# Up projection of a diffusion block on one core: the upper weight part multiplies both token parts in one matmul of 512 columns

## The chip, the cores and the metric

The kernel runs on one core of one Trainium2 chip. The metric is the time of one execution on the device, in microseconds. Five engines work side by side and meet through semaphores: TensorE (PE for its matmuls, PEld for its weight loads), VectorE (DVE), ScalarE (ACT), GpSimd (POOL) and SyncE (SP), whose queue issues the weight transfers here.

## The reference

One layer of a diffusion block over 256 latent tokens with 256 context tokens, model width 2048. The part that the change touches is the MLP, with a hidden width of 8192:

```python
def squared_relu_mlp(h, w_up, w_down):
    return jnp.square(jax.nn.relu(h @ w_up)) @ w_down

hm = modulate(rms_norm(x, norm_mlp_w[layer]), sh_m, sc_m)
x = x + g_m * squared_relu_mlp(hm, w_mlp_up[layer], w_mlp_down[layer])
```

Ahead of it stand the adaLN products (`w_ada`), the input projection, a windowed attention with a pooling mixer beside it, and the output projection.

## The kernel before, in words

All large products are float32, computed as three products of two-part operands: a number is split into a rounded upper part (`hi`, type float32r) and the rest (`lo`), and `mm3` (L278) adds a[0]·b[0] (L280), a[0]·b[1] (L281) and a[1]·b[0] (L282) into one PSUM bank. Here a is the stationary operand (128 x 128, loaded into TensorE by a LDWEIGHTS of its own ahead of each matmul), b the moving one.

Weights come as one ordered stream of 1 MB tiles (`WeightStream`, L52): SP issues the loads five tiles deep (`N_RAW`), and each tile is split in two halves of 128 x 1024, the upper part by ScalarE (`hi`, L89), the lower part by VectorE, now and then GpSimd (`lo`, L91), six halves deep (`N_HALF`). A half's buffer comes free when TensorE has used the half, so a split usually starts when TensorE lets go of an old half.

The MLP stands at the end, from about 424 us on. The 8192 hidden columns go in 16 groups of 512; a group has four sums `m` of 128 hidden columns by 256 tokens and runs over 16 row blocks `k`. The first three groups are computed together (`first_up_groups`, L873). The other 13 go through `up_group` (L863): for each of four weight tiles, for each `m`, for each of the tile's four row blocks, one `mm3` with the weights stationary and the tokens' parts `mhi`, `mlo` (128 x 256 each) moving. So a position (group, `k`, `m`) costs three matmuls of 256 columns, and the weights' upper part is loaded twice. The tokens' parts are allocated by `parts` (L565), which also serves the attention and the pooling, and written by `modulate_m` (L841).

`activation` (L852) makes a group's four sums into the operand of the down projection: ScalarE's Relu out of PSUM (L857), VectorE's square (L858), then the two parts `ahi` (ScalarE, L859) and `alo` (VectorE, L860). `down_group` (L902) multiplies two groups' activations, as stationary operands, with 512 columns of `w_down`, 48 matmuls of 512 columns. The loop at L929 goes over blocks `b`: for b = 0 the first two groups, for b = 1 the third one and one `up_group`, for b = 2 to 7 two `up_group`s each, and each time four `down_group`s (`dg`).

A scheduler sets the order on each engine: it may move an instruction ahead of others of its engine in the program's text where data permit, so a matmul whose operand comes late can stand behind later ones.

Of the kernel before, what the change touches and what calls it, by code (L numbers as in the profile page):

```python
# [15 lines left out]
P = 128  # L16
D = 2048
# [10 lines left out]
# among the first so many tiles of the stream, GpSimd computes every third lower part  # L28
POOL_SPLITS = 140

# adaLN parts beyond the attention's shift and scale, in order of use: 512 columns of its gate ("g")
# or 256 of the MLP's scale and of its shift ("m"); the engine that multiplies them; and between
# which steps their tiles go, four for each
# [11 lines left out]
# groups of row blocks of w_out in their order of use: those of the pooling are ready first  # L45
OUT_ORDER = (0, 1, 2, 3)

# row blocks of w_in that are used at a time: (first, number)
# [3 lines left out]
class WeightStream:  # L52
    """One ordered stream of float32 weight tiles of four blocks [128, 512].

    Tiles are loaded in order, N_RAW deep. Those of the main products are split
    ahead of their use, two blocks at a time, into two float32r parts
    (hi + lo == w exactly).
    """
# [6 lines left out]
    def add(self, kind, *loads, halves=2):  # L65
        """loads: (view of the tile, source)."""
        if kind == "w":
            self.halves += [(len(self.items), h) for h in range(halves)]
        self.items.append((kind, loads, halves))
# [25 lines left out]
    def next(self, kind):  # L95
        """The next tile: the raw one, or W(j, cols) -> the parts of block j."""
        i = self.pos
        assert self.items[i][0] == kind, (i, self.items[i][0], kind)
        self.pos += 1
        self.load_to(i + N_RAW)  # L100
        self.split_to(self.n_used + N_AHEAD)
        raw = self.raw.pop(i)
        if kind != "w":
            return raw
        n = self.items[i][2]
        self.n_used += n
        halves = [self.split.pop((i, h)) for h in range(n)]

        def parts(j, cols=slice(0, 512)):
            hi, lo = halves[j // 2]  # L110
            return hi[:, j % 2, cols], lo[:, j % 2, cols]

        return parts
# [3 lines left out]
def kernel(  # L117
# [17 lines left out]
    # ------------------------------------------------------------ weight stream  # L135
# [15 lines left out]
    # the input projection's schedule, with the first shift and scale in pairs of row blocks  # L151
# [50 lines left out]
    # the last group's q goes before the attention, its u beside it  # L202
# [45 lines left out]
    # ------------------------------------------------------------ constants  # L248
# [10 lines left out]
    # ------------------------------------------------------------ small helpers  # L259
    def rstd(pool, ss, n):  # L260
        """1 / sqrt(ss / D + EPS) of ss [128, n], or of the sum of two."""
# [16 lines left out]
    def mm3(ps, a, b, first, last):  # L278
        """ps (+)= a^T b with a and b in two parts each."""
        nc.tensor.matmul(ps, a[0], b[0], start=first, stop=False, skip_group_check=True)  # L280
        nc.tensor.matmul(ps, a[0], b[1], start=False, stop=False, skip_group_check=True)  # L281
        nc.tensor.matmul(ps, a[1], b[0], start=False, stop=last, skip_group_check=True)  # L282

    def ada_pe(finish):
        """Steps that multiply silu(c), silu(c_ctx) with 512 columns of w_ada on TensorE; a last one calls finish(e).

        Rows 32 j and 32 j + 1 of e hold partial sums.
        """
# [18 lines left out]
    def ada_dve(finish):  # L307
        """The same for silu(c) alone on VectorE: the sum of the rows of e is the result."""
# [14 lines left out]
    def ada_cols(e, weights):  # L323
        """e^T weights: the result with the columns on the partitions, PSUM [128, 4, 2]."""
# [5 lines left out]
    def ada_scale(dst, ps, bc, wc):  # L330
        """dst [128, n, 2] = w * (1 + scale)."""
# [6 lines left out]
    # ------------------------------------------------------------ norm of x and ctx  # L338
# [38 lines left out]
    def ada_attn(c_):  # L377
        """Scale and shift of the row blocks 2 c_ and 2 c_ + 1."""
# [11 lines left out]
    def normalize(i):  # L390
        """Tokens 128 i .. of x | ctx over their root mean square, transposed."""
# [24 lines left out]
    # ------------------------------------------------------------ input projection  # L416
# [15 lines left out]
    def modulated(c_, streams=(0, 1)):  # L432
        """The input projection's operand, in two parts, of the row blocks 2 c_ and 2 c_ + 1."""
# [79 lines left out]
    def run_late(n):  # L513
        """The next n steps; a chunk is finished one step after its last."""
        for _ in range(n):
            f = next(late_iter, None)
            while late_finish:
                late_finish.pop()()
            if f:
                f()  # L520
# [42 lines left out]
    # ------------------------------------------------------------ attention and pooling  # L563
# [4 lines left out]
    def parts(j):  # L568
        pool = mixa if j < 8 else mixb
        hi = pool.tile([P, T], F32R, tag=f"mhi{j}", name=f"mhi{j}", bufs=1)  # L570
        lo = pool.tile([P, T], F32R, tag=f"mlo{j}", name=f"mlo{j}", bufs=1)
        return hi, lo
# [10 lines left out]
    # masks of the two blocks: keys after the query (block 0), keys before it (block 1)  # L583
# [9 lines left out]
    def rotate(t):  # L593
        """Axial rotary of t [128, n, 256], in place."""
# [9 lines left out]
    def split_keys(g):  # L604
        """The two parts of the keys of group g, each on both halves of the partitions."""
# [10 lines left out]
    def split_queries(cc):  # L616
        """For the heads 2 cc and 2 cc + 1, one part on each half of the partitions."""
# [8 lines left out]
    def pool_mean(g):  # L626
        """Window mean minus the token itself, in place of u."""
# [25 lines left out]
    def pool_project(g):  # L653
# [7 lines left out]
        for d in range(2):  # L661
            mhi, mlo = parts(8 + 2 * g + d)
# [5 lines left out]
    # the attention of the heads 2 cc and 2 cc + 1 for the block qb of 128 queries, in stages  # L668
    class Unit:
# [14 lines left out]
        def maxima(self):  # L684
            """Masks, and the negated maxima of the scaled scores and the sink."""
# [35 lines left out]
    def attend(cc):  # L721
# [6 lines left out]
        mhi, mlo = parts(cc)  # L728
# [53 lines left out]
    # ------------------------------------------------------------ output projection  # L782
# [53 lines left out]
    # ------------------------------------------------------------ MLP  # L836
# [4 lines left out]
    def modulate_m(kg):  # L841
        """The up projection's operand, in two parts, of four row blocks."""
        for j in range(4):
# [3 lines left out]
            hi, lo = parts(k)  # L847
            nc.scalar.activation(hi, v, AF.Identity, bias=sm[:, k, 0:1])
            nc.vector.scalar_tensor_tensor(lo, v, sm[:, k, 0:1], hi.bitcast(F32), ALU.add, ALU.subtract)
            hm.append((hi, lo))  # L850

    def activation(pss):  # L852
        ahi = mp.tile([P, 4, T], F32R, tag="ahi", name="ahi", bufs=3)
        alo = mp.tile([P, 4, T], F32R, tag="alo", name="alo", bufs=3)
        for m in range(4):
            t = mp.tile([P, T], F32, tag="act", name="act", bufs=2)
            nc.scalar.activation(t, pss[m], AF.Relu)  # L857
            nc.vector.tensor_tensor(t, t, t, ALU.mult)  # L858
# [4 lines left out]
    def up_group():  # L863
        pss = [bank("ps_up")[:, 0:T] for _ in range(4)]
        for kg in range(4):
            w = S.next("w")
            for m in range(4):
                for j in range(4):
                    k = 4 * kg + j
                    mm3(pss[m], w(j, slice(P * m, P * m + P)), hm[k], k == 0, k == KC - 1)  # L870
        return activation(pss)

    def first_up_groups():  # L873
        """Three groups at once, by row blocks, so that the last shifts and scales can come late.

        Two sums share a bank: the first product of the bank starts both.
        """
# [24 lines left out]
    def down_group(b, dg, acts, done=None):  # L902
        """Sums of 8 row blocks for 512 columns; done: called with each token block's as it is ready."""
# [37 lines left out]
    # last block: x2 + g * y is ready before its sums are  # L941
# [50 lines left out]
def _shape_constants():  # L992
    """Rotary tables [128, 2, 256] (cos, signed sin) and window size over tokens in the window at the two ends."""
# [40 lines left out]
```

## Time and profile before

| | |
|---|---|
| median of 3 runs | 1180.92 us (1180.76 to 1180.92) |
| span of the profiled execution | 1180.8 us |
| PE busy | 1128.4 us (96%) |
| DVE busy | 806.4 us (68%) |
| ACT busy | 509.2 us (43%) |
| granted TensorE clock, mean | 0.982 |

The profiled execution's span and the runs' median are 0.1 us apart; the profile names no time of its own beyond the span. A matmul's duration in a row (0.28 us for 256 columns) is longer than the distance from its start to the next one's start, since matmuls overlap in the array: what a stream of them costs is read from the starts. Clock 1.00 is 2.4 GHz, 0.50 is 1.2 GHz.

### The profile page before, as it was taken

How to read it: one execution, taken by the hardware profiler on the slowest of the kernel's cores; microseconds unless marked ns; L12 is line 12 of the kernel's file. 1: busy time of each engine (PE TensorE's matmuls, PEld its weight loads, DVE VectorE, ACT ScalarE, POOL GpSimd, SP SyncE). 2: the span in 40 equal slices, each digit the busy share in tenths (PEclk: the TensorE clock that was granted, in tenths of full speed). 3: DMA queues.
4: the chain of work that ended last, by engine and by line, in shares of the span. 5: the costliest groups of instructions: out<-in, count | busy, mean ns of one | idle time of the engine just before them, and what ended most of it. 6: DMA issues, size and time to landing. Idle time of an engine off the chain costs nothing.

```text
span 1180.8 us, 17728 instructions
## 1 busy us (share of the span) xinstructions
PE 1128.4 (96%) x7140; PEld 952.2 (81%) x7140; DVE 806.4 (68%) x1203; ACT 509.2 (43%) x760; POOL 145.8 (12%) x98
## 2 busy tenths in 40 slices
PE   3999999989999979999999999999999999999996
PEld 2767788746588769988989989989989989988984
DVE  4645468988698888897765765774554554576576
ACT  4633233277633433365434434533533533543452
POOL 1111123610143312320000000000000000000001
PEclk9899999999999979899999999999999999999998
DMA  9999898577898899968675775775566555565532
GB/s 338 312 336 342 279 326 276 178 268 263 272 350 278 288 328 322 319 229 284 243 278 179 249 263 184 254 262 178 179 191 193 187 178 181 185 195 189 179 107 72
DMA packets 174017, 286.75 MB, mean 243 GB/s; under 512 B 5608, under 2 KB 72352, under 8 KB 172784
## 3 DMA queue, kind: packets, MB, share of 16 engines
q1 hardware_dynamic: 172800, 279.55, 70.7%
q0 software_dynamic: 848, 5.55, 1.3%
q8 instruction: 56, 0.92, 0.3%
q10 hardware_dynamic: 288, 0.52, 0.1%
q14 instruction: 25, 0.20, 0.0%
HBM read 283.50 MB, written 2.10 MB: 242 GB/s over the span
## 4 chain that ended last, share of the span: by engine, by line
PE 74%; DVE 13%; DMA 7%; issue 3%; ACT 1%; SPq 1%; POOL 1%; DVEq 0%; ACTq 0%
PE ps_d L282 10%; PE ps_d L281 10%; PE ps_d L280 10%; PE ps_up L282 9%; PE ps_up L280 9%; PE ps_up L281 9%; PE ps_ada L297 4%; DVE ada_v L319 4%; DVE lo L91 4%; DMA raw<-in_w_in_dram 2%; PE ps_qu L280 2%; DMA raw<-in_w_mlp_up_dram 2%; DMA raw<-in_w_out_dram 2%; PE ps_qu L282 2%; PE ps_qu L281 2%
## 5 line engine op out<-in xcount | busy, mean ns | idle before, releaser
L91 DVE TENSOR_TENSOR lo<-raw,hi 128x1024 fp32r<-128x1024 f32 x293 | 376.7, 1300 | 233.5 <-ACT hi L89 233.3
L89 ACT CAST hi<-raw 128x1024 fp32r<-128x1024 f32 x330 | 337.7, 1049 | 416.6 <-PE ps_d L282 159.4
L280 PE MATMUL ps_up<-mhi,hi 128*128 128x256 f32 x1024 | 292.0, 287 | 0.6 <-ACT hi L89 0.6
L282 PE MATMUL ps_up<-mhi,lo 128*128 128x256 f32 x1024 | 289.5, 285 | 1.4 <-DVE lo L91 1.4
L281 PE MATMUL ps_up<-mlo,hi 128*128 128x256 f32 x1024 | 290.1, 284 | 0.0
L281 PE MATMUL ps_d<-lo,ahi 128*128 128x512 f32 x512 | 200.5, 394 | 0.0
L280 PE MATMUL ps_d<-hi,ahi 128*128 128x512 f32 x512 | 200.5, 394 | 0.0
L280 PEld LDWEIGHTS ps_up<-mhi,hi 128*128 128x128 f32 x1024 | 197.4, 193 | 2.7 <-issue 1.8
L282 PE MATMUL ps_d<-hi,alo 128*128 128x512 f32 x512 | 199.5, 395 | 0.0
L282 PEld LDWEIGHTS ps_up<-mhi,lo 128*128 128x128 f32 x1024 | 196.8, 193 | 2.2 <-DVE lo L91 2.1
L281 PEld LDWEIGHTS ps_up<-mlo,hi 128*128 128x128 f32 x1024 | 197.5, 193 | 1.1 <-issue 1.0
L319 DVE SCALAR_TENSOR_TENSOR ada_v<-raw,c_sil,ada_v 128x512 f32<-128x512 f32 x135 | 124.7, 923 | 22.0 <-DMA raw<-in_w_ada_dram 20.1
L91 POOL TENSOR_TENSOR lo<-raw,hi 128x1024 fp32r<-128x1024 f32 x37 | 95.4, 2580 | 336.4 <-ACT hi L89 316.9
L282 PEld LDWEIGHTS ps_d<-hi,alo 128*128 128x128 f32 x512 | 96.5, 188 | 22.4
L280 PEld LDWEIGHTS ps_d<-hi,ahi 128*128 128x128 f32 x512 | 96.5, 188 | 22.2
L281 PEld LDWEIGHTS ps_d<-lo,ahi 128*128 128x128 f32 x512 | 96.5, 188 | 22.1
L280 PE MATMUL ps_qu<-hhi,hi 128*128 128x256 f32 x256 | 75.6, 296 | 5.9 <-ACT hhi L447 5.9
L297 PE MATMUL ps_ada<-raw,c_sil 128*32 128x512 f32 x480 | 74.3, 629 | 2.0 <-DMA raw<-in_w_ada_dram 1.9
L281 PE MATMUL ps_qu<-hlo,hi 128*128 128x256 f32 x256 | 72.7, 285 | 0.0
L282 PE MATMUL ps_qu<-hhi,lo 128*128 128x256 f32 x256 | 72.1, 285 | 0.0
L950 POOL DMA_DIRECT2D fw<-in_final_norm_w_dram x1 | 0.6, 571 | 576.3 <-DVE lo L91 576.3
L280 PEld LDWEIGHTS ps_qu<-hhi,hi 128*128 128x128 f32 x256 | 49.4, 193 | 24.4 <-issue 11.5
(189 smaller groups left out, 1275.2 us busy)
## 6 DMA issues: line engine op xcount, KB each, us to landing
raw<-in_w_ada_dram SPq DMA_DIRECT2D x128, 512.0 KB, 7.7
raw<-in_w_mlp_up_dram SPq DMA_DIRECT2D x64, 1024.0 KB, 5.5
raw<-in_w_mlp_down_dram SPq DMA_DIRECT2D x64, 1024.0 KB, 5.1
raw<-in_w_ada_dram SPq DMA_DIRECT2D x32, 1024.0 KB, 6.6
raw<-in_w_in_dram SPq DMA_DIRECT2D x19, 1024.0 KB, 6.7
raw<-in_w_out_dram SPq DMA_DIRECT2D x16, 1024.0 KB, 7.0
xnat<-in_x_dram SPq DMA_DIRECT2D x2, 1024.0 KB, 6.1
xnat<-in_ctx_dram SPq DMA_DIRECT2D x2, 1024.0 KB, 12.2
```

Of the source, the lines that this page charges most:

```text
L89: nc.scalar.copy(hi, raw)
L91: eng.tensor_tensor(lo, raw, hi.bitcast(F32), ALU.subtract)
L280: nc.tensor.matmul(ps, a[0], b[0], start=first, stop=False, skip_group_check=True)
L281: nc.tensor.matmul(ps, a[0], b[1], start=False, stop=False, skip_group_check=True)
L282: nc.tensor.matmul(ps, a[1], b[0], start=False, stop=last, skip_group_check=True)
L297: nc.tensor.matmul(ps[32 * j : 32 * j + 32, :], c_sil[:, 4 * kg + j, :], raw[:, j, :], start=(kg == 0), stop=(kg == 3), tile_position=(0, ...
L319: nc.vector.scalar_tensor_tensor(box["e"], raw[:, j, :], sc, box["e"], ALU.mult, ALU.add)
L950: nc.gpsimd.dma_start(out=fw, in_=final_w.partition_broadcast(P))
```

## The change

The two parts of a token block become one tile of 128 x 2 x 256 (`both`), `hi` in its first 256 columns and `lo` in the next. In `up_group` the weights' upper part multiplies the whole tile in one matmul of 512 columns, which fills a bank: the product with `hi` in the first half, that with `lo` in the second. The weights' lower part multiplies `hi` (256 columns) into the first half. `activation` adds the halves: ScalarE copies the second half to SBUF, VectorE adds the first one, and a second instruction of VectorE takes the positive part and squares it; the split into `ahi` and `alo` stays. `first_up_groups` keeps `mm3` and the old branch of `activation`. Comments and docstrings fall away too.

```diff
     def parts(j):
         pool = mixa if j < 8 else mixb
-        hi = pool.tile([P, T], F32R, tag=f"mhi{j}", name=f"mhi{j}", bufs=1)
-        lo = pool.tile([P, T], F32R, tag=f"mlo{j}", name=f"mlo{j}", bufs=1)
-        return hi, lo
+        both = pool.tile([P, 2, T], F32R, tag=f"mx{j}", name=f"mx{j}", bufs=1)
+        return both[:, 0, :], both[:, 1, :], both.rearrange("p a t -> p (a t)")
...
-            hi, lo = parts(k)
+            hi, lo, both = parts(k)
...
-            hm.append((hi, lo))
+            hm.append((hi, lo, both))
...
-            nc.scalar.activation(t, pss[m], AF.Relu)
-            nc.vector.tensor_tensor(t, t, t, ALU.mult)
+            if pss[m].shape[1] == T:
+                nc.scalar.activation(t, pss[m], AF.Relu)
+                nc.vector.tensor_tensor(t, t, t, ALU.mult)
+            else:
+                nc.scalar.copy(t, pss[m][:, T : 2 * T])
+                nc.vector.tensor_tensor(t, pss[m][:, 0:T], t, ALU.add)
+                nc.vector.scalar_tensor_tensor(t, t, 0.0, t, ALU.max, ALU.mult)
...
     def up_group():
-        pss = [bank("ps_up")[:, 0:T] for _ in range(4)]
+
+        pss = [bank("ps_up") for _ in range(4)]
         for kg in range(4):
             w = S.next("w")
             for m in range(4):
                 for j in range(4):
                     k = 4 * kg + j
-                    mm3(pss[m], w(j, slice(P * m, P * m + P)), hm[k], k == 0, k == KC - 1)
+                    hi, lo = w(j, slice(P * m, P * m + P))
+                    nc.tensor.matmul(pss[m], hi, hm[k][2], start=k == 0, stop=False, skip_group_check=True)
+                    nc.tensor.matmul(pss[m][:, 0:T], lo, hm[k][0], start=False, stop=k == KC - 1, skip_group_check=True)
         return activation(pss)
```

The order of every engine up to the first `up_group` is the one of before; from there on it moves at three kinds of places. First TensorE inside an `up_group` (`ps_up` is a sum, `hi` and `lo` the weights' parts, `mhi12`, `mlo12`, `mx2` and so on the tokens'), before:

```order
L280 MATMUL ps_up_7835<-mhi12_4703,hi_7897 128x256
L281 MATMUL ps_up_7835<-mlo12_4704,hi_7897 128x256
L282 MATMUL ps_up_7835<-mhi12_4703,lo_7898 128x256
L280 MATMUL ps_up_7835<-mhi13_4708,hi_7897 128x256
L281 MATMUL ps_up_7835<-mlo13_4709,hi_7897 128x256
L282 MATMUL ps_up_7835<-mhi13_4708,lo_7898 128x256
```

and now:

```order
L876 MATMUL ps_up_7930<-mx2_4037,hi_7863 128x512
L877 MATMUL ps_up_7930<-mx2_4037,lo_7864 128x256
L876 MATMUL ps_up_7930<-mx3_4041,hi_7863 128x512
L877 MATMUL ps_up_7930<-mx3_4041,lo_7864 128x256
L876 MATMUL ps_up_7927<-mx4_4230,hi_7893 128x512 [waits Activation_49]
L877 MATMUL ps_up_7927<-mx4_4230,lo_7894 128x256 [waits DVE_49]
```

Two matmuls stand where three stood, of lengths that alternate. Second, VectorE around the end of a block's second `up_group`, from b = 4 on; before:

```order
L858 TENSOR_TENSOR act<-act 128x256 x2
L860 TENSOR_TENSOR alo<-act,ahi 128x256 x2
L858 TENSOR_TENSOR act<-act 128x256
L91 TENSOR_TENSOR lo<-raw,hi 128x1024
L860 TENSOR_TENSOR alo<-act,ahi 128x256
L91 TENSOR_TENSOR lo<-raw,hi 128x1024
L858 TENSOR_TENSOR act<-act 128x256
L860 TENSOR_TENSOR alo<-act,ahi 128x256
```

and now:

```order
L861 TENSOR_TENSOR act<-ps_up,act 128x256 x2
L862 SCALAR_TENSOR_TENSOR act<-act 128x256 x2
L864 TENSOR_TENSOR alo<-act,ahi 128x256 x2
L91 TENSOR_TENSOR lo<-raw,hi 128x1024
L861 TENSOR_TENSOR act<-ps_up,act 128x256
L91 TENSOR_TENSOR lo<-raw,hi 128x1024
L861 TENSOR_TENSOR act<-ps_up,act 128x256
L862 SCALAR_TENSOR_TENSOR act<-act 128x256 x2
L864 TENSOR_TENSOR alo<-act,ahi 128x256
L91 TENSOR_TENSOR lo<-raw,hi 128x1024
L864 TENSOR_TENSOR alo<-act,ahi 128x256
```

The fourth sum's `alo` is last in both; now four more instructions and one more weight split of `lo` stand in the stretch. Third, TensorE in the `down_group`s right behind: the last first use of the second group's `alo` (row block 3, the row with the last DVE wait) stood 40 matmuls behind the first `ps_d`, before:

```order
L280 MATMUL ps_d1_8896<-hi_8817,ahi_8873 128x512
L281 MATMUL ps_d1_8896<-lo_8818,ahi_8873 128x512
L282 MATMUL ps_d1_8896<-hi_8817,alo_8874 128x512
L280 MATMUL ps_d1_8896<-hi_8817,ahi_8873 128x512
L280 MATMUL ps_d0_8895<-hi_8821,ahi_8873 128x512 [waits Activation_49]
L281 MATMUL ps_d0_8895<-lo_8822,ahi_8873 128x512
L281 MATMUL ps_d1_8896<-lo_8818,ahi_8873 128x512
L282 MATMUL ps_d0_8895<-hi_8821,alo_8874 128x512 [waits DVE_49]
```

and now 51 behind it, with matmuls of the next 512 columns (`ps_d0_8395`) drawn in ahead:

```order
L280 MATMUL ps_d0_8323<-hi_8261,ahi_8297 128x512 [waits Activation_49]
L281 MATMUL ps_d0_8323<-lo_8262,ahi_8297 128x512
L280 MATMUL ps_d1_8324<-hi_8261,ahi_8297 128x512
L281 MATMUL ps_d1_8324<-lo_8262,ahi_8297 128x512
L280 MATMUL ps_d0_8395<-hi_8327,ahi_8099 128x512
L281 MATMUL ps_d0_8395<-lo_8328,ahi_8099 128x512
L282 MATMUL ps_d0_8323<-hi_8261,alo_8298 128x512 [waits DVE_49]
```

The place is 51 matmuls behind for b = 4 to 7, 60 for b = 2 and 3 (before: 41), 55 for b = 1 (before: 40). GpSimd's and SP's orders do not move.

## Rows read from the trace of the kernel before

**Rows 1.** The page: busy time of the engines, and the chain by line.

```profile
PE 1128.4 (96%) x7140; PEld 952.2 (81%) x7140; DVE 806.4 (68%) x1203; ACT 509.2 (43%) x760; POOL 145.8 (12%) x98
...
PE ps_d L282 10%; PE ps_d L281 10%; PE ps_d L280 10%; PE ps_up L282 9%; PE ps_up L280 9%; PE ps_up L281 9%; PE ps_ada L297 4%; DVE ada_v L319 4%; DVE lo L91 4%; DMA raw<-in_w_in_dram 2%; PE ps_qu L280 2%; DMA raw<-in_w_mlp_up_dram 2%; DMA raw<-in_w_out_dram 2%; PE ps_qu L282 2%; PE ps_qu L281 2%
```

**Rows 2.** Windows of the MLP: length; each engine's busy time (instructions); clock; DMA.

```profile
core 0: us, PE busy (x) PEld busy (x) DVE busy (x) ACT busy (x) POOL busy (x), PEclk, DMA share, GB/s
622.74:714.28 91.54, 91.54 (x580) 82.61 (x579) 59.95 (x74) 38.52 (x49) 0.00 (x0) 1.00 0.69 230
```

**Rows 3.** Windows, instructions on `ps_up` alone: two groups of b = 5.

```profile
896.90:942.98 46.08, 46.08 (x384) 46.02 (x383) 2.68 (x7) 1.00 0.56 184
```

**Rows 4.** Windows, instructions on `ps_d` alone: the four `down_group`s of b = 5.

```profile
942.98:987.50 44.52, 44.52 (x192) 35.98 (x192) 4.82 (x7) 0.00 (x0) 1.00 0.60 187
```

**Rows 5.** Timeline, PE: both ends of that stretch (start us, us, operation).

```profile
942.86 0.28 PE L282 MATMUL ps_up<-mhi,lo 128*128 128x256 f32 x1
942.98 0.39 PE L280 MATMUL ps_d<-hi,ahi 128*128 128x512 f32 x1
...
987.36 0.40 PE L282 MATMUL ps_d<-hi,alo 128*128 128x512 f32 x1
987.59 0.28 PE L280 MATMUL ps_up<-mhi,hi 128*128 128x256 f32 x1
```

**Rows 6.** Timeline, PE: output projection, first and last of 44 matmuls.

```profile
340.09 0.39 PE L282 MATMUL ps_w<-hi,mlo 128*128 128x512 f32 x1
...
349.84 0.39 PE L280 MATMUL ps_w<-hi,mhi 128*128 128x512 f32 x1
```

**Rows 7.** Timeline, PE: values of the input projection, first and last of 11 matmuls.

```profile
148.04 0.28 PE L281 MATMUL ps_v<-lo,hhi 128*128 128x256 f32 x1
...
149.17 0.28 PE L282 MATMUL ps_v<-hi,hlo 128*128 128x256 f32 x1
```

**Rows 8.** Timeline, PE: one matmul of 512, six of 256, then 512 again.

```profile
95.20 0.39 PE L280 MATMUL ps_k<-hhi,hi 128*128 128x512 f32 x1
95.43 0.28 PE L281 MATMUL ps_v<-lo,hhi 128*128 128x256 f32 x1
...
96.14 0.40 PE L281 MATMUL ps_k<-hlo,hi 128*128 128x512 f32 x1
96.38 0.40 PE L282 MATMUL ps_k<-hhi,lo 128*128 128x512 f32 x1
```

**Rows 9.** Groups by line and shape: busy us, mean ns, idle before.

```profile
L857 ACT ACTIVATE act<-ps_up 128x256 f32<-128x256 f32 x64 | 24.3, 382 | 33.4 <-PE ps_up L282 24.1 <-DVE alo L860 9.0 <-PE ps_up L281 0.2
L858 DVE TENSOR_TENSOR act<-act 128x256 f32<-128x256 f32 x64 | 28.5, 455 | 9.5 <-ACT act L857 8.3
L849 DVE SCALAR_TENSOR_TENSOR mlo<-x2T,sm,mhi 128x256 fp32r<-128x256 f32 x16 | 6.9, 477 | 0.2 <-ACT mhi L848 0.2
L730 DVE TENSOR_TENSOR mlo<-ps_o,mhi 128x256 fp32r<-128x256 f32 x8 | 3.3, 418 | 3.6 <-ACT mhi L729 3.6
L729 ACT CAST mhi<-ps_o 128x256 fp32r<-128x256 f32 x8 | 3.0, 378 | 9.8 <-PE ps_o L726 9.1 <-DMA raw<-in_w_ada_dram 0.7
```

**Rows 10.** Timeline, DVE and ACT: the activation of b = 2, whose sums end at 669.21.

```profile
668.62 1.05 ACT L89 CAST hi<-raw 128x1024 fp32r<-128x1024 f32 x1 [0.27 <-PE ps_up L281]
673.58 1.05 ACT L89 CAST hi<-raw 128x1024 fp32r<-128x1024 f32 x1 [0.42 <-PE ps_d L282]
...
671.17 1.22 DVE L91 TENSOR_TENSOR lo<-raw,hi 128x1024 fp32r<-128x1024 f32 x1
674.18 0.42 DVE L860 TENSOR_TENSOR alo<-act,ahi 128x256 fp32r<-128x256 f32 x1
674.51 0.75 DVE L319 SCALAR_TENSOR_TENSOR ada_v<-raw,c_sil,ada_v 128x512 f32<-128x512 f32 x1
```

**Rows 11.** PE behind a wait in the first groups, and a window at half clock.

```profile
489.11 1.02 PE L327 MATMUL ps_adac<-ones,ada_v 128*128 128x2 f32 x8 [0.98 <-DVE ada_v L319]
490.50:497.30 6.80, 6.26 (x30) 5.97 (x29) 5.42 (x10) 0.91 (x2) 0.68 (x1) 0.50 1.00 352
```

More of the change, by code (lines that the diff above doesn't have):

```diff
@@ L661, in pool_project @@
         for d in range(2):
-            mhi, mlo = parts(8 + 2 * g + d)
+            mhi, mlo, _ = parts(8 + 2 * g + d)
             sc = cols[:, 64 + 2 * g + d : 65 + 2 * g + d]
@@ L727, in attend @@
                                  start=(k == 0), stop=(k == 3), tile_position=(0, 64 * i))
-        mhi, mlo = parts(cc)
+        mhi, mlo, _ = parts(cc)
         nc.scalar.copy(mhi, ps[:, 0:T])
```

## The prediction

> **What bounds the kernel now.** I read the page's busy time first, then its chain of waits: TensorE is busy 96% of the span, and the chain that ended last is mostly TensorE, with `ps_up` (27%) and `ps_d` (30%) as its largest parts [rows 1]. The page stands for the whole span, so I looked next at windows inside the MLP. From 622.74 to 714.28 us, a whole block of it, PE is busy for all of 91.54 us at clock 1.00, while VectorE has 59.95 and ScalarE 38.52 us of work and the DMA engines are at 0.69 [rows 2]. Nothing is waited for there: what a matmul costs from start to start is what the block costs.
>
> That cost is in the starts. Two groups are 384 matmuls of 256 columns in 46.08 us [rows 3], 120.0 ns each. The four `down_group`s of the same block are 192 of 512 columns from 942.98 to 987.59 us [rows 4, 5], 44.61 us, 232.3 ns each. At 2.4 GHz the columns alone would take 106.7 and 213.3 ns, so a matmul carries some 13 to 19 ns beside its columns, and a matmul less is worth that much, though the columns stay: 3 x 256 before, 512 + 256 now.
>
> The spacing is not one number. In the output projection 512 columns take (349.84 - 340.09) / 43 = 226.7 ns [rows 6], 13.3 above the columns, as with the 120.0 of `ps_up`; in a stretch of the value projection 256 columns take (149.17 - 148.04) / 10 = 113 ns [rows 7], 6 above them. All are at full clock and without idle time between, and go on unchanged through their stretches, so the fixed part depends on which operands a stream reads. The output projection reads the same buffers as the up projection (weight parts and the tiles of `parts`), with the roles of moving and stationary exchanged; so I take its 226.7 for the new matmul.
>
> **The change, part by part.**
>
> TensorE. 13 groups x 16 row blocks x 4 sums = 832 positions go through `up_group`. Before, one costs 3 x 120.0 = 360.0 ns [rows 3]. Now it costs one matmul of 512 and one of 256: 226.7 + 120.0 = 346.7 ns, 13.3 less. 832 x 13.3 ns = 11.1 us, all on the path, since PE has no idle time in the stage. The trace has one short stretch in which the lengths alternate without a pause: one of 512, six of 256, one of 512, from 95.20 to 96.38 us [rows 8], 1.18 us, where 2 x 226.7 + 6 x 120.0 makes 1.17. Changing the length twice cost nothing that two decimals show. The price of a pair that alternates every time is not in the trace. Bounds: 226.7 + 113 = 340 ns, saving 16.6 us, if the matmul of 256 takes the spacing of [rows 7]; and 240 + 120 = 360 ns, saving nothing, if every 512 behind a 256 took the 0.24 us from 96.14 to 96.38 [rows 8]. Between them lies 232.3 + 120.0 = 352.3 ns, the spacing of the down projection [rows 4], saving 6.4 us. I take 346.7, of which each half is a row on these buffers.
>
> The Trainium skill speaks against most of this gain: its page "TensorE: Matmul & The Clock Gate", section "Back-to-back issue gap", puts a warm matmul's spacing at its columns over 2.4 GHz plus about 2.5 ns. By that rule the estimate for 832 matmuls less is 2.1 us, and the time 1178.8. The rows do not agree: 120.0 stands where the rule has 109.2. The rival "small fixed part" below is worked out from rows.
>
> Weight loads. 832 fewer LDWEIGHTS. They overlap the matmuls (PEld is busy 46.02 of 46.08 us beside them [rows 3]), so I count nothing beyond the matmuls' own spacing, in which they are included.
>
> ScalarE. The Relu out of PSUM, 382 ns, becomes a copy out of PSUM; the copy of `ps_o` of the same shape takes 378 [rows 9]. Zero.
>
> VectorE. The square of 455 ns becomes an addition with one operand in PSUM, as L730 does in 418 ns, and a scalar_tensor_tensor, as L849 does in 477 [rows 9]: 440 ns more for each sum, 52 sums, 22.9 us more busy time. In a block it is 8 x 0.44 = 3.5 us on top of 59.95 in 91.54 [rows 2], so the engine keeps up. Its cover is the work of TensorE between a group's end and the first use of its activation, and that has to be checked at the last group of each block.
>
> There the sums of b = 2 end at 669.21 us, and the last `alo` ended at 674.18 + 0.42 = 674.60 [rows 10], 5.4 us later. By the order, now four additions (4 x 0.42) and the longer second instruction (4 x 0.02) join, and one more split of a weight half (1.22 [rows 10]) for b = 4 to 7: at most 5.4 + 3.0 = 8.4 us. The order puts the first use of that `alo` 51 matmuls behind the start of `ps_d`, 51 x 0.2323 = 11.8 us. Slack 3.4 us. For b = 2 and 3 two more splits join: 5.4 + 1.8 + 2.4 = 9.6 us against 60 x 0.2323 = 13.9. For b = 1, with as much added, 9.6 against 55 x 0.2323 = 12.8. So I cost this at nothing. If the cover were gone, each us late would cost one us at each of seven boundaries.
>
> Splits. ScalarE's `hi` and VectorE's `lo` of the stream stand in the same queues, and a few of them start 1 to 3 us later. They start when TensorE lets go of a half (the two `hi` of [rows 10]), six halves deep, five halves or nearly 14 us ahead of use (a half is 12 matmuls of 0.2323 us). Zero.
>
> PSUM. A group's bank now comes free after VectorE's addition and not after ScalarE's Relu, about 1 us later; eight banks are used in turn and the next write to a bank of the block's second group is in the third `down_group`, 22 us on. Zero. The merged tile of `parts` leaves every order up to the first `up_group` as it was: zero.
>
> Sum: 1180.8 - 11.1 = 1169.7 us of span. The span lies 0.1 us below the runs' median of 1180.92, so the time that I forecast is 1169.8 us.
>
> **The rivals.**
>
> Down-like spacing: the 512 takes 232.3 ns as in [rows 4]; 1180.9 - 6.4 = 1174.5. For it: `ps_d` is the stage next to it, and moves operands of the same length. Against it: the buffers of [rows 6].
>
> Short spacing: the pair falls to 340 ns, 1180.9 - 16.6 = 1164.3. For it: [rows 7] has 113 ns. Against it: `ps_up` itself has 120.0 without exception.
>
> Small fixed part, so that the change doesn't do what it says: a switch of length costs what the missing matmul saves, 0.36 us a pair by the 0.24 of [rows 8]. Then it is 1180.9, and no change as long as a pair stays above 357 ns. The rule of the Trainium skill above ends in the same place. Against it: the sum of [rows 8] leaves no room for two such switches.
>
> Late activation, the slower side: VectorE's longer chain ends behind the first use of `alo`, and TensorE stands at seven boundaries (b = 1 to 7). It decides from 3.4 us beyond my sum on; the gain is gone when each wait is 11.1 / 7 = 1.6 us, that is 5 us beyond it. At 2 us each it is 14 - 11.1 = 2.9 us slower, 1183.8. A clock that falls makes it worse: behind a wait of PE of about 1 us and a stretch of tiny matmuls, the window from 490.50 to 497.30 ran at 0.50, the 1.2 GHz level [rows 11], which is 3.4 us lost each time. For it: VectorE gets 22.9 us more work, in an order it must keep. Against it: the slack of 3.4 to 4.3 us above.
>
> **How the numbers follow.** Forecast (near 346.7 ns a pair) 0.60; down-like spacing 0.18; short spacing 0.09; small fixed part 0.08; late activation 0.05. About 0.2% (2.4 us) is what a measurement of this kernel can tell from no change. The first three are faster by more: 0.87; same 0.08; slower 0.05. The range runs from the short spacing, 1164, to 1177, which holds the down-like spacing with a us or two of waits at the boundaries and leaves out the two last cases.
>
> **What would show it.** In the profile of the changed kernel: L876 and L877 832 times each; the distance from one L876 to the next, 0.347 us in the middle of a group, is the forecast itself (0.340, 0.352 and 0.360 are its rivals); two groups take 44.4 us in place of 46.08; `ps_d` stays at 232.3 ns. No idle time of PE behind `alo` or `ahi` in the first two `down_group`s of a block, and clock 1.00 there. VectorE's busy time is about 829 us. I would be wrong if the pair comes near 0.36, if `ps_d`'s spacing moves, or if PE waits for VectorE at the boundaries.

## The result and the profile after

| | before | after |
|---|---|---|
| median | 1180.92 us (1180.76 to 1183.69, 5 runs) | 1172.09 us (1171.78 to 1176.11, 5 runs) |
| span of the profiled execution | 1180.8 us | 1170.0 us |
| that execution's own time | not recorded | 1171.78 us |

The ratio is 0.9929, with a 95% interval of 0.9910 to 0.9948: the change is 8.8 us faster between the medians. Forecast were 1169.8 us, in a range of 1164 to 1177. In every execution with both numbers on record the time is 1.7 to 1.9 us above the span, so the profiled execution of the kernel before took an estimated 1182.6 us, some 1.7 us more than its median.

The page of the changed kernel, busy time of each engine and the chain of waits, answers to [rows 1]:

```profile
PE 1120.1 (96%) x6308; PEld 905.4 (77%) x6308; DVE 820.6 (70%) x1255; ACT 507.4 (43%) x760; POOL 145.2 (12%) x98
...
PE 81%; DVE 11%; DMA 3%; issue 2%; ACT 1%; SPq 1%; DVEq 0%; ACTq 0%
PE ps_up L876 17%; PE ps_d L281 10%; PE ps_d L282 10%; PE ps_d L280 10%; PE ps_up L877 8%; PE ps_ada L297 4%; DVE ada_v L319 3%; DVE lo L91 3%; PE ps_qu L280 2%; PE ps_qu L282 2%; PE ps_qu L281 2%; PE ps_o L725 2%; DMA raw<-in_w_in_dram 1%; PE tp_p L714 1%; PE ps_w L280 1%
```

TensorE has 832 instructions less and still bounds the kernel. `ps_up` fell from 27% of the chain to 25% (17 and 8), and VectorE has 14 us more work.

The two spans differ by 10.8 us, but not all of that is the change. The timeline of PE gives the cut: the first `ps_up` of b = 1 and the first `ps_d` of b = 7. In the kernel before:

```profile
554.24 0.68 PE L280 MATMUL ps_up<-mhi,hi 128*128 128x256 f32 x1
...
1124.35 0.39 PE L280 MATMUL ps_d<-hi,ahi 128*128 128x512 f32 x1
```

and in the changed one:

```profile
551.28 0.80 PE L876 MATMUL ps_up<-mx,hi 128*128 128x512 f32 x1
...
1113.73 0.39 PE L280 MATMUL ps_d<-hi,ahi 128*128 128x512 f32 x1
```

Between them lie all 832 changed positions. This stage took 570.11 us before and 562.45 after: 7.66 us less. A further 2.96 us lie ahead of it, where the order of TensorE is as before, and 0.15 behind it. All runs below are read by this stage, because the part ahead of it varies: with the same order of TensorE ahead, the stage starts between 550.2 and 555.6 us in the profiles of this document.

Windows over single stretches (columns: stretch, its length, busy time and count of PE, PEld, DVE and ACT, clock, DMA share, GB/s). First, instructions on `ps_up` alone, b = 2 to 7, answering to [rows 3]:

```profile
619.37:665.00 45.63, 45.63 (x256) 39.28 (x256) 2.09 (x5) 2.23 (x6) 1.00 0.57 193
710.25:755.03 44.78, 44.78 (x256) 39.17 (x256) 2.09 (x5) 2.23 (x6) 1.00 0.58 196
800.11:845.74 45.63, 45.63 (x256) 39.24 (x256) 2.52 (x6) 2.23 (x6) 1.00 0.57 179
890.53:934.91 44.38, 44.38 (x256) 39.01 (x255) 2.52 (x6) 2.22 (x6) 1.00 0.58 187
979.53:1023.91 44.38, 44.38 (x256) 38.66 (x255) 2.52 (x6) 2.22 (x6) 1.00 0.58 187
1068.52:1113.73 45.21, 45.21 (x256) 39.08 (x255) 2.51 (x6) 2.23 (x6) 1.00 0.57 185
```

128 pairs in 44.38 us are 346.7 ns a pair, the forecast to the tenth. The first three rows hold 0.40 us more for the start behind `ps_gm`, as these blocks did before (46.47 us there, 46.07 in the later ones). Without that, b = 3, 5 and 6 run at 346.7 ns and b = 2, 4 and 7 at 353.2; the group of b = 1 is of the slower kind too. No block lies between the two. The timeline of PE shows both levels without any pause; first b = 5, six pairs, then b = 4, seven:

```profile
899.90 0.39 PE L876 MATMUL ps_up<-mx,hi 128*128 128x512 f32 x1
900.13 0.28 PE L877 MATMUL ps_up<-mx,lo 128*128 128x256 f32 x1
...
901.98 0.39 PE L876 MATMUL ps_up<-mx,hi 128*128 128x512 f32 x1
...
809.70 0.40 PE L876 MATMUL ps_up<-mx,hi 128*128 128x512 f32 x1
809.93 0.28 PE L877 MATMUL ps_up<-mx,lo 128*128 128x256 f32 x1
...
812.17 0.40 PE L876 MATMUL ps_up<-mx,hi 128*128 128x512 f32 x1
```

2.08 us over six is 347 ns, 2.47 over seven 353. The slower kind is not slower evenly: from start to start, its pairs take about 350, 350 and 361 ns in turn.

Windows of `ps_d` in b = 5, b = 2 and b = 4, in this order, answer to [rows 4, 5]:

```profile
934.91:979.53 44.62, 44.61 (x192) 36.00 (x192) 4.73 (x7) 0.00 (x0) 1.00 0.59 192
664.99:709.79 44.80, 44.80 (x192) 35.86 (x192) 4.71 (x7) 0.00 (x0) 1.00 0.82 270
845.73:890.53 44.80, 44.80 (x192) 35.85 (x192) 4.73 (x7) 0.00 (x0) 1.00 0.60 190
```

So the down projection has two levels too: 232.4 ns a matmul in four of the stage's six stretches, as before, and 233.3 in the other two. The timeline of VectorE behind b = 2, whose sums end at 665.00, answers to [rows 10]:

```profile
672.13 0.42 DVE L864 TENSOR_TENSOR alo<-act,ahi 128x256 fp32r<-128x256 f32 x1
...
674.95 0.42 DVE L864 TENSOR_TENSOR alo<-act,ahi 128x256 fp32r<-128x256 f32 x1
```

The groups of the new activation (mean ns behind the busy us), with the twelve squares that the first groups keep (L858), answer to [rows 9]:

```profile
L861 DVE TENSOR_TENSOR act<-ps_up,act 128x256 f32<-128x256 f32 x52 | 21.6, 419 | 2.5 <-ACT act L860 2.3
L862 DVE SCALAR_TENSOR_TENSOR act<-act 128x256 f32<-128x256 f32 x52 | 19.7, 415 | 0.0
L858 DVE TENSOR_TENSOR act<-act 128x256 f32<-128x256 f32 x12 | 6.9, 598 | 1.7 <-ACT act L857 1.7
L860 ACT COPY act<-ps_up 128x256 f32<-128x256 f32 x52 | 19.3, 371 | 20.4 <-PE ps_up L877 16.0 <-DVE alo L864 4.4
```

The last `alo` of b = 2 is ready 10.4 us behind the sums, 3.5 us ahead of its first use, 60 matmuls of `ps_d` or 13.9 us behind the sums. In the whole stage PE waits for nothing.

### The profile page after: what moved, and what is told of

The parts are those of the page before. It is cut to its first block, busy times and chain, and to the rows that moved or that the text cites. A ratio compares the mean times of both kernels' runs of the same rounds, so it can differ in the third digit from the quotient of the medians.

```text
span 1170.0 us, 16111 instructions
## 1 busy us (share of the span) xinstructions
PE 1120.1 (96%) x6308; PEld 905.4 (77%) x6308; DVE 820.6 (70%) x1255; ACT 507.4 (43%) x760; POOL 145.2 (12%) x98
## 3 DMA queue, kind: packets, MB, share of 16 engines
q0 software_dynamic: 848, 5.55, 1.3%
## 4 chain that ended last, share of the span: by engine, by line
PE 81%; DVE 11%; DMA 3%; issue 2%; ACT 1%; SPq 1%; DVEq 0%; ACTq 0%
PE ps_up L876 17%; PE ps_d L281 10%; PE ps_d L282 10%; PE ps_d L280 10%; PE ps_up L877 8%; PE ps_ada L297 4%; DVE ada_v L319 3%; DVE lo L91 3%; PE ps_qu L280 2%; PE ps_qu L282 2%; PE ps_qu L281 2%; PE ps_o L725 2%; DMA raw<-in_w_in_dram 1%; PE tp_p L714 1%; PE ps_w L280 1%
## 5 line engine op out<-in xcount | busy, mean ns | idle before, releaser
L876 PE MATMUL ps_up<-mx,hi 128*128 128x512 f32 x832 | 293.3, 397 | 0.0
L877 PE MATMUL ps_up<-mx,lo 128*128 128x256 f32 x832 | 233.0, 280 | 0.0
L876 PEld LDWEIGHTS ps_up<-mx,hi 128*128 128x128 f32 x832 | 156.1, 188 | 37.9 <-issue 1.0
L877 PEld LDWEIGHTS ps_up<-mx,lo 128*128 128x128 f32 x832 | 157.0, 189 | 1.1 <-issue 1.0
L282 PE MATMUL ps_up<-mx,lo 128*128 128x256 f32 x192 | 53.1, 285 | 4.6 <-DVE lo L91 4.6
L281 PE MATMUL ps_up<-mx,hi 128*128 128x256 f32 x192 | 53.7, 283 | 0.0
```

The lines of the kernel that those rows point to most:

```text
L876: nc.tensor.matmul(pss[m], hi, hm[k][2], start=k == 0, stop=False, skip_group_check=True)
L877: nc.tensor.matmul(pss[m][:, 0:T], lo, hm[k][0], start=False, stop=k == KC - 1, skip_group_check=True)
```

## The experiments

Open after the result: why half of the pairs cost 6.6 ns more than the other half, and whether the activation is really free. Theory A: the spacing is set by how the stream of matmuls runs, where it starts, where the column count changes, what it was doing before; a stream keeps its level until something disturbs it. Theory B: it is set by the data's place, the buffers that happen to serve a block. From e6_shift on a second pair, C and D, asks the same of the down projection. In the expectations of e1_again, e2_blocked and e3_three C stands for something else, waits of TensorE for the activation, and in those of e2_blocked, c1_two and c2_tile D stands for a cost of the alternation itself.

**e1_again**: the changed kernel, unchanged, once more.

> The changed kernel once more, unchanged. Its first profile has two levels for a pair of L876 and L877, 346.7 ns in the blocks b = 3, 5, 6 and 353.3 ns in b = 1, 2, 4, 7, each from the block's start to its end. Theory A (the level is a matter of how the stream of a block starts, and is kept): 1171 to 1173 us, both levels again and no third one, and the blocks that have them may be others; each of the blocks b = 2 to 7 that goes over to the other level moves the time by 128 x 6.7 ns = 0.85 us. Theory B (the level belongs to the buffers that a block reads): the same blocks have the same levels again, 1171.9 us. Theory C (part of the forecast gain is lost in waits of TensorE for the activation): idle time of PE behind alo or ahi at the seven boundaries, some 0.4 us each.

1172.70 us (1170.03 to 1173.68, 6 runs) against 1180.66 of before; 0.9924 (0.9903 to 0.9945). The stage is 562.45 us again and each of its 13 stretches is the same to 0.01 us. The levels are no noise: the same program fell into the same ones. This alone does not tell A from B, since both allow it.

**e3_three**: the merged tile and the new activation, with the three matmuls of 256 kept.

```
-    nc.tensor.matmul(pss[m], hi, hm[k][2], start=k == 0, ...)
+    nc.tensor.matmul(pss[m][:, 0:T], hi, hm[k][0], start=k == 0, ...)
+    nc.tensor.matmul(pss[m][:, T : 2 * T], hi, hm[k][1], start=False, ...)
```

> The merged tile and the new activation, but three matmuls of 256 columns as before (the second one into the second half of the bank). If all of the gain is in the matmuls and the activation costs nothing: 1180.9 us, no change from the kernel before, spacing 120.0 ns, VectorE some 14 to 23 us busier, no idle time of PE at the boundaries. Theory C: 1182 to 1184 us, slower than before by what the changed kernel is short of its forecast.

1179.9 us against 1180.66; 0.9993 (0.9982 to 1.0005). The timeline of PE at the ends of the stage:

```profile
550.98 0.68 PE L876 MATMUL ps_up<-mx,hi 128*128 128x256 f32 x1
...
1121.08 0.39 PE L280 MATMUL ps_d<-hi,ahi 128*128 128x512 f32 x1
```

570.10 us, the stage of before within its last digit. The activation and VectorE's added work cost nothing, and the whole gain is TensorE's; waits for the activation fall as a cause. The stage also starts at 550.98 here, 3.26 us earlier than in the profile of before although nothing ahead of it is cheaper: the 2.96 us of the changed kernel are of that kind.

**e4_wide_only**: the new matmul alone. It leaves out the product with the weights' lower part.

```
-    nc.tensor.matmul(pss[m], hi, hm[k][2], start=k == 0, stop=False, ...)
-    nc.tensor.matmul(pss[m][:, 0:T], lo, hm[k][0], ...)
+    nc.tensor.matmul(pss[m], hi, hm[k][2], start=k == 0, stop=k == KC - 1, ...)
```

> Leaves out the product with the weights' lower part, so that an up group is a stream of matmuls of 512 columns alone, weights stationary and the merged tokens' tile moving. By the forecast's term: 226.7 ns each, as in the output projection. If the operands of this stage bring the down projection's spacing: 232.3. The stage is bound by less, since a tile now lasts 16 x 4 x 0.227 = 3.6 us on TensorE: where the loads (1 MB a tile) or the splits can't follow, PE waits for them, and the spacing is to be read from a stretch without waits.

The window of `ps_up` in b = 5:

```profile
835.40:864.43 29.03, 29.03 (x128) 23.84 (x127) 2.02 (x6) 2.10 (x6) 1.00 0.81 268
```

29.03 / 128 = 226.8 ns. The forecast's price of the matmul of 512, taken from the output projection [rows 6], holds for a stream of its own, as 120.0 does for the matmul of 256 in e3_three. What comes on top belongs to their alternation.

**e5_flip and c3_rev**: the order within the pairs. e5_flip exchanges the two matmuls of one pair at the start of tiles 2 to 4 of each group, on the same buffers:

```
+    flip = k > 0 and m == 0 and j == 0
+    if flip:  # the matmul of 256 first
```

> The changed kernel with one pair of matmuls exchanged at the start of the second, third and fourth weight tile of each group (the 256 before the 512; accumulation in any order). The work is the same. Theory A (the level is kept from the stream's start until something disturbs it): at some of these places the level changes within a group, and the time lies between 1170 (all at 346.7) and 1173 (all at 353.3). Theory B (buffers): the levels stay as in the changed kernel, and hold from a block's start to its end, 1172 us.

c3_rev has the matmul of 256 first in every pair but those of the first row block of a sum:

```
+    if k > 0:
+        nc.tensor.matmul(pss[m][:, 0:T], lo, hm[k][0], ...)
     nc.tensor.matmul(pss[m], hi, hm[k][2], start=k == 0, ...)
```

> The pair the other way round, 256 before 512, from the second row block on; in the first tile the two orders meet, from the second tile on the stream alternates as in the changed kernel, on the same buffers. Theory A: from the second tile on one level per block, 346.7 or 353.3, but not in the blocks of the changed kernel (b = 3, 5, 6 low), since the phase at which the stream starts is another one. Theory B (buffers): b = 3, 5, 6 at 346.7, b = 1, 2, 4, 7 at 353.3 again.

e5_flip: 1175.48 us (1174.59 to 1177.44, 7 runs), 0.9955 (0.9939 to 0.9971), stage 564.31. The time lies above the 1170 to 1173 us expected: the stage is 1.86 us longer than the changed kernel's, and the rest of the 3.39 us between the medians lies outside it. Windows of `ps_up` in its b = 4, the first tile of 16 pairs and the second, which begins with the exchanged pair:

```profile
804.38:810.33 5.95, 5.95 (x32) 5.05 (x33) 0.00 (x0) 0.00 (x0) 1.00 0.53 164
810.33:815.97 5.64, 5.64 (x34) 4.90 (x33) 0.00 (x0) 0.00 (x0) 1.00 0.51 175
```

Less the 0.40 us of the start the first tile is 5.55 us, 346.9 ns a pair, in a block that ran at 353 in the changed kernel. From the exchanged pair on it is 352.5. All blocks from b = 2 on behave alike, b = 3, 5 and 6 too. Each of them follows a `ps_d` stretch of 44.80 us here, as only b = 3 and 5 do in the changed kernel; b = 1 follows one of 44.62 us and starts slow in both kernels. This fits A, but is no rule: b = 6 of the changed kernel is fast behind 44.62 us. c3_rev (1177.94 us, one run) has 351 to 354 ns in all blocks and a stage of 564.24. So a block's buffers don't choose its level, and a single exchanged pair can move it: A stands and B falls, as far as the up projection goes. The later exchanges of e5_flip did not move it back.

**e2_blocked, c1_two, c2_tile and c2_timed**: fewer changes of length. Matmuls of one length stand together: 4 and 4 in e2_blocked, 2 and 2 in c1_two, 16 and 16 in c2_tile (once more as c2_timed), whose edit is

```
+    for part in range(2):
         for m in range(4):
             for j in range(4):
+                if part == 0:  # the 16 of 512 columns
                     nc.tensor.matmul(pss[m], hi, hm[k][2], ...)
+                else:          # the 16 of 256
                     nc.tensor.matmul(pss[m][:, 0:T], lo, hm[k][0], ...)
```

> For each sum the four matmuls of 512 columns first, then the four of 256, so that the length changes twice in eight matmuls and not eight times. If the alternation is what brings the level of 353.3 (theory D): all blocks at 346.7 a pair or near it (four of 512 at 226.7, four of 256 at 120.0), 448 pairs x 6.7 = 3.0 us less than the changed kernel, some 1169 us. Theory A: a block settles into some level all the same; 512 at 226.7 or 232.3 and 256 at 113 to 120, between 340 and 353 a pair, 1168 to 1173 us. Theory C: as the changed kernel, 1172 us, since the activation is the same.

> By halves of a tile: two matmuls of 512, then two of 256. Theory A (a stream settles by its own phase at the start; what it reads does not decide): one level that repeats with the pattern, the same in each tile of a block, between 340 and 353 ns a pair; where 346.7 holds in all blocks the stage from the second up group to the last block is 3 us shorter than in the changed kernel. Theory D (alternation costs; fewer changes of length are better): between the changed kernel's mean of 350 and the 346.7 of the lower level, and below the 350.8 of the version with four and four.

> By whole tiles: sixteen matmuls of 512, then sixteen of 256, so that the length changes twice in 32. Theory D: the lowest of all the orders, 226.7 + 120.0 = 346.7 ns a pair in all blocks. Theory A: long streams settle, 512 at 226.7 or 232.3 and 256 at 113 to 120, that is 340 to 353 a pair; the version with four and four has 350.8 because it never settles. A tile's halves come free later, at its end: if that matters, PE waits for hi or lo.

> The kernel c2_tile once more, timed in five rounds against the kernel before: in each weight tile the 16 matmuls of 512 columns stand ahead of the 16 of 256. Its single run had a stage of 560.15 us against 562.45 of the changed kernel and 570.11 of the kernel before. Theory A (the spacing is set where the stream starts or changes its column count, so fewer changes cost less): the stage again 560.15 us within 0.05, and 1180.7 - 9.96 = 1170.7 us in the median, up to 2 us either way by the stages ahead of the MLP, ratio 0.989 to 0.993; that is 2.3 us under the changed kernel, hardly more than the two can be told apart by. Theory B (buffers set the spacing): no gain over the changed kernel, 1172 to 1173 us.

| matmuls of a length together | ns a pair | stage, us | time, us | ratio |
|---|---|---|---|---|
| 1 (after) | 346.7 or 353.2 | 562.45 | 1172.09 | 0.9929 (0.9910 to 0.9948) |
| 2 (c1_two) | 348.3 | 560.54 | 1171.41, one run | |
| 4 (e2_blocked) | 350.8 | 562.47 | 1172.62 | 0.9929 (0.9910 to 0.9947) |
| 16 (c2_tile) | 347.9 | 560.15 | 1168.56, one run | |
| 16 (c2_timed) | 347.9 | 560.15 | 1170.53 | 0.9921 (0.9907 to 0.9936) |

Where matmuls of one length stand together, all blocks have one spacing, within 0.3 ns. The single runs c2_tile and c2_timed, of one kernel on two chips, have the same stage. In c2_timed the timeline of PE shows where the rest sits:

```profile
903.62 2.08 PE L880 MATMUL ps_up<-mx,lo 128*128 128x256 f32 x16
905.53 3.82 PE L878 MATMUL ps_up<-mx,hi 128*128 128x512 f32 x16
909.18 2.08 PE L880 MATMUL ps_up<-mx,lo 128*128 128x256 f32 x16
```

In steps of 1 ns, in which the trace holds them, 16 of 512 take 3.654 us, 27 ns more than 16 x 226.7; 16 of 256 take 1.913, 7 ns less than 16 x 120.0. Those 20 ns are the 1.2 ns by which each of 16 pairs lies above 346.7. The first few starts behind a change carry that, and the streams then run at their own 226.7 and 120.0. The order of the costs isn't that of the counts, though: 2 and 2 is cheaper than 4 and 4, and the 350.8 of 4 and 4 misses the 346.7 that was expected if the alternation alone cost. What rule makes it so stays open. The gain over the changed kernel, 2.30 us of the stage, is real by the trace and too small for the medians to tell.

**e6_shift, c6_both and c7_pair**: the place of an operand. The forecast had read from [rows 4, 6, 7] that the fixed part depends on which operands a stream reads. The clearest case is the down projection: 232.3 ns, with `ahi` and `alo` as the loaded operand, against 226.7. By the program's addresses, which no trace holds, counted modulo 512 bytes, these tiles stand at 288; the weights that stream past them stand at 160, as do both operands of the output and the up projection. e6_shift moves the tiles by 128 bytes, with nothing changed in TensorE's order. The other tiles behind `x2` in SBUF, `act`, `ada_v` and `y` among them, move along:

```
     x2 = xp.tile([P, 2, D], F32, name="x2")
+    pad = xp.tile([P, 32], F32, name="pad")
+    nc.gpsimd.memset(pad, 0.0)
```

> The changed kernel with all activation tiles of the MLP (ahi and alo among them) moved by 128 bytes in SBUF, by a tile of 32 columns that nothing reads; every instruction of TensorE stands in the same order on the same data. It asks where the long spacing of the down products comes from (232.3 ns for one matmul of 128x512, with ahi and alo as the loaded operand) against the 226.7 ns of the output projection's and of the pure stream of the up products. Theory C, the place of the loaded tile in its partition adds to the spacing: the down stretches change by a measurable amount, at best from 44.6 and 45.1 us to 192 x 226.7 = 43.5 us, that is 7 to 10 us off the stage's 562.45 us between the first and the last down stretch. Theory D, the spacing belongs to the pattern of the stream and not to addresses: the seven down stretches stay within 0.2 us of the 44.60 to 45.26 us of the changed kernel. In both the up pairs keep one of their two levels, 346.7 or 353.3 ns, in each block.

c6_both takes 80 columns in place of 32, and c2_tile's order.

> The order of c2_tile (in each weight tile the 16 matmuls of 512 columns ahead of the 16 of 256) together with the activation tiles of the MLP moved by 320 bytes instead of the 128 of e6_shift, by a tile of 80 columns that nothing reads. Counted modulo 512 bytes the loaded operand of the down products then stands at 480; it stood at 288 in the changed kernel (232.4 ns a matmul) and at 160 in e6_shift (226.7 ns). In the value projection a loaded operand at 480 went with 113 ns for 256 columns where one at 160 went with 120. Theory C1, the place modulo 512 bytes sets the spacing, with 480 the better by the same 6.5 ns: 220.2 ns a matmul, down stretches of 42.3 us, a stage near 560.15 - 16 = 544 us and a median near 1170.5 - 18 = 1152 us. Theory C2, 480 is only another place that doesn't disturb: 226.7 ns as in e6_shift, stretches of 43.6 to 44.0 us, stage 552.8 us, median near 1163 us. Theory C3, only 160, the place of the other operand, is free of the extra time: 232 ns or more, stage 560 us or above, median 1170 us or above. In each the up pairs keep c2_tile's 347.9 ns.

c7_pair takes 32 again, and c2_tile's order.

> The order of c2_tile (in each weight tile the 16 matmuls of 512 columns ahead of the 16 of 256) with the move of e6_shift by 128 bytes, so that the down products' loaded operand and the one that streams stand at the same place modulo 512 bytes, 160. c6_both, with 480 against 160, kept 232 ns. Theory C3 (the two operands' places against each other set the spacing of the down products, and the order in the tile that of the up products, each by itself): down stretches of 43.6 to 44.0 us as in e6_shift, up pairs of 347.9 ns as in c2_tile, a stage of 560.15 - 7.35 = 552.8 us, and a median of 1170.5 - 7.35 - 1.1 (the last down stretch, which is behind the stage) = 1162 us, ratio 0.982 to 0.987. Rival D2 (e6_shift's short stretches came from how its streams happened to begin, not from the place): down stretches of 44.6 us or above somewhere, stage 555 us or above, median 1165 us or above.

Windows of `ps_d` in b = 5, first of e6_shift, then c6_both, then c7_pair:

```profile
929.53:973.12 43.59, 43.59 (x192) 35.86 (x192) 4.73 (x7) 0.00 (x0) 1.00 0.61 194
```

```profile
932.81:977.61 44.80, 44.80 (x192) 35.91 (x192) 4.73 (x7) 0.00 (x0) 1.00 0.59 185
```

```profile
930.34:973.89 43.55, 43.55 (x192) 35.87 (x192) 4.72 (x7) 0.00 (x0) 1.00 0.60 190
```

227.0 and 226.8 ns a matmul where the loaded operand stands at 160, 233.3 at 480. At 288 there were 232.4 ns before, and both 232.4 and 233.3 in the changed kernel; in e5_flip, at 288 as well, every stretch of the stage has 233.3, here b = 5:

```profile
939.59:984.39 44.80, 44.80 (x192) 35.86 (x192) 4.74 (x7) 0.00 (x0) 1.00 0.59 190
```

So 480 has not been shown to be dearer than 288: its 233.3 is a level that 288 has too. C is right that the place counts, D falls; of the guesses on how, C1 and C2 fall and C3 stands. In c7_pair all seven down stretches, that of b = 0 included, are of 43.55 us, so D2 falls. That 480 went with 113 ns in the value projection was no guide: equal places are the cheap ones of the three tried. That it is the loaded operand, and not another tile that moved along, is argued, since TensorE reads none of the others in these stretches; no run moves it alone. e6_shift's stage is 555.37 us, 7.08 less than the changed kernel's, and its one run 1164.26 us. With the down stretches' ends the levels of the up pairs moved as well, windows of `ps_up` in b = 4 and 5 of e6_shift:

```profile
795.98:840.76 44.78, 44.78 (x256) 39.18 (x256) 2.52 (x6) 2.24 (x6) 1.00 0.55 182
884.33:929.53 45.20, 45.20 (x256) 39.12 (x255) 2.52 (x6) 2.24 (x6) 1.00 0.56 185
```

b = 4 is now of the fast kind (44.38 and the 0.40 of the start) and b = 5 of the slow, the reverse of the changed kernel, on the same code for the up projection. That fits A once more: what ran before decides.

c6_both: 1172.12 us (1169.70 to 1174.40, 6 runs), 0.9926 (0.9907 to 0.9944), stage 561.29. c7_pair: 1163.60 us (1161.62 to 1165.35, 4 runs) against 1180.09, ratio 0.9856 (0.9836 to 0.9875), stage 553.75, 0.95 above what I had expected, since I had counted seven down stretches, of which the stage holds six. Its up pairs keep 347.9 ns, its down stretches 43.55 us (44.01 with the `ps_gm` behind them): the two gains add. c7_pair is faster than both kernels of this study, by 16.5 us than the one before, timed beside it, and by 8.5 than the changed one, timed apart.

## Why the prediction was right

**The spacing of the pair** is the step that was mis-sized. It said 346.7 ns for all 832 pairs, saving 11.1 us. 384 pairs have exactly that; the other 448 cost 353.2, near the rival's 352.3, though for another reason than the rival gave. 384 x 13.3 + 448 x 6.8 = 8.2 us; the seven `ps_up` stretches of the stage fell from 301.04 to 293.02, 8.02. The step that failed is "changing the length twice cost nothing that two decimals show" [rows 8]: one stretch with two changes, in steps of 0.01 us, can't rule out 6.6 ns a pair, and 6.6 ns is half of the saving at stake. In the trace's steps of 1 ns the first 256 of that stretch takes 113 and the 512 behind the six takes 234, so the two changes cancelled there. What makes a stream take the slower level stays open. The bounds of 340 and 360 ns held. The time by itself favours nobody: 1172.09 us is 2.3 above the forecast and 2.4 below the rival's 1174.5, and only the spacing of the pairs tells them apart.

**Each half by its own row** was right for streams of one length: 226.8 ns measured alone in e4_wide_only, 120.0 in e3_three's unchanged stage. In the fast pairs only the sum holds: the mean distances from start to start are 230.0 and 116.7 ns in b = 5, and 231.6 and 115.1 in b = 6. No run shows why they still add up to 346.7, so the exact agreement may be luck.

The formula of the Trainium skill, page "TensorE: Matmul & The Clock Gate", section "Back-to-back issue gap", columns over 2.4 GHz and about 2.5 ns, would give an estimate of 215.8 ns for the 512 and a saving of 2.1 us. The section gives it for an isolated matmul and says of a stream of weight loads and matmuls that both set the spacing, which the prediction left out. The rows measured 226.8, and 7.66 us of stage.

**`ps_d` stays** at 232.3 ns: nearly. Its six stretches in the stage, with the `ps_gm` behind three of them, rose from 269.07 to 269.43 us, so 0.37 us of the 8.02 went back; with it the stage's 7.66 is complete. All of it lies in b = 2 and 4, at 233.3 ns behind slow pairs. By the prediction's own words a spacing of `ps_d` that moves is a sign of being wrong; it moved there, by a size that the time doesn't show.

**VectorE and the activation.** The 455 ns of [rows 9] is a mean of 64 squares, and the 12 that stay take 598 each; if they did so before, the 52 that changed took an estimated 422. These became 419 + 415, 412 more a sum where I had 440. The page's total rose by 14.2 us, not 22.9: busy time counts overlapping instructions once, and other groups moved a little. The last `alo` of b = 2 came 10.4 us behind the sums, beyond my 9.6, and still 3.5 us ahead of its use. The cover held, as e3_three shows too: its stage has the same activation and lost nothing.

**Clock, splits, PSUM, weight loads**: the granted clock is 1.00 in each window of the stage, and PE has no idle time there; nothing of these shows. Each matmul less is also a weight load less, so no run here tells which of the two the saved 13.3 ns belong to.

**The time.** 1180.8 - 11.1 was a forecast of the span, and the span came out at 1170.0, which looks better than the step was: 2.96 us of it are the stages ahead, which vary. That agreement is luck. So is the 0.1 us that the prediction found between span and median: it compared the span of one execution with the time of others, while every later run has 1.7 to 1.9 us between its own two. The forecast of the time doesn't suffer, as 1180.92 - 11.1 is 1169.8 too. The median, 2.3 us above the forecast, is the fairer reading.

The forecast's remark that the fixed part depends on the operands was right, and could have been worth more than the change: the six down stretches of the stage lost 6.63 us in e6_shift against the changed kernel, and 6.39 in c7_pair against c2_timed. Why [rows 7] has 113 ns stays open.

## What to carry to other kernels

Where TensorE never waits, price a merged matmul by measured start-to-start distances and check the alternation itself over a long stretch: neighbours of another length can cost a few ns a pair, and that was a quarter of the forecast gain here. Compare kernels by the one stage that changed, from matmul to matmul; it repeated to 0.01 us here while whole runs moved by 2 us and more. When two streams of equal length have different spacings, look at where their operands stand before rewriting either.

## What the hardware showed beyond that

A stream that alternates 512 and 256 columns has two exact spacings, 346.7 and 353.2 ns a pair; it keeps one for a whole block, the same in both profiles of the changed kernel, and one exchanged pair, or another spacing of the matmuls ahead of it, can move it to the other. A shift of the loaded tiles by 128 bytes took a stream of 512 columns from 232.4 to 226.8 ns; with one by 320 bytes it ran at 233.3, a level that it also had unshifted. Three places were tried; whether the distance of the two operands or the place by itself counts, and what in the chip makes it so, was not told apart.
